# A hybrid mLSTM and gated-delta block on one core: last corrections of a head group behind the next gate's first weight split, later first phases, a sigmoid moved

## The chip, the cores and the metric

The kernel runs on one core of one Trainium2 chip. The metric is the device time of one execution in microseconds (us). The core has a matmul engine (TensorE, PE), a vector engine (VectorE, DVE), an activation engine (ScalarE, ACT), a general engine (GpSimd, POOL) and a sync engine that issues DMAs (SyncE, SP). Each engine works through its own instructions in order.

## The reference

One block of a bidirectional hybrid encoder over 256 tokens of width 2048, in fp32:

```python
mod = c_act @ ada_w + ada_b           # shift, scale, gate of both sub-layers
h = rms_norm(x, norm_mix_w) * (1 + scale_m) + shift_m
proj = h @ w_in                       # a_q a_k a_v a_o a_i a_f | b_qkv b_z b_beta b_a | merge
h_a = bidirectional(mlstm_chunkwise, (q_a, k_a, v_a), ...)          # 4 heads, 512 wide
y_a = (sigmoid(a_o) * rms_norm(h_a)) @ w_branch_a
o_b = bidirectional(gated_delta_chunkwise, (q_b, k_b, v_b), ...)    # 16 heads, 128 wide
y_b = (rms_norm(o_b) * silu(b_z)) @ w_branch_b
x = x + gate_m * ((g_a * y_a + g_b * y_b) @ w_out)
x = x + gate_f * SwiGLU(rms_norm(x) * (1 + scale_f) + shift_f)
```

A final RMSNorm follows. The change touches the gated delta rule of branch B (GDN: 16 heads), its output gate z, and the output gate of branch A, sigmoid(a_o).

## The kernel before, in words

**Every projection** is a product with weights from memory, done in three passes of reduced-precision matmuls. A job loads a weight tile (`raw`, three buffers in all), ACT copies a part of it to `wh`, DVE subtracts to `wl` (three buffers each), and PE adds wh x h-high, wh x h-low and wl x h-high into PSUM. There are two kinds of job. A `tjob` (L195) takes halves of 128x1024: load at L206, wh at L209, wl at L211, twelve 128x512 matmuls at L230 to L232. An `fjob` takes 24 matmuls of 128x256 for a half, with wh at L182 and the matmuls at L187 to L189. A job is a generator that gives one half per step. When a tjob has the argument `early`, its first `early` halves are split at its first step and pinned to the program's order by `order`; other instructions may be moved by the scheduler.

**The GDN** runs over four groups of four heads. For a group, `gdn_invert` inverts 32x32 blocks on DVE: a memset at L687, then steps of a multiplication (L692) and an addition (L698) on the tile uu, which a DMA brings in. Then two pairs of heads run the chain `gdn_phase2`: products p1 to p4 (L743 to L783), then pa, pb and pc (L795, L796, L807), then po (L817 to L822) and a norm. At its last step the chain transposes the result on PE (px, L829), ACT evicts px to obt (L833), and a DMA stores obt to ob_d (L834).

**The order around it.** While a pair's chain runs, `stream` (L875) works off the projections b_job of two heads of the next group, and then `gdn_phase1` of them: vf comes from ACT at L337, PE transposes it to vps at L601, ACT evicts it, and ks follows at L630. The list todo counts down how many pieces later a head's next phase comes. When nothing of the stream is left, `fill(1)` takes the next half from a list of other projections (v, o, q and k of branch A, and the merge gates ma and mb). The tables after, second and last say how many pieces come between two steps of the chain. So these halves are what PE does while a chain waits for DVE or ACT. The gate z of the next group is `z_job`, put at the head of the fills once both pairs are done, with `early` as 0.

**After the last group** the mLSTM of the first two heads runs. For a head, sgo is loaded by POOL (L939), PE sums pden (L950), ACT makes dn from it (L952), PE makes ph (L966), ACT and DVE turn it into hs (L968, L969), ACT squares it (L970) and takes a square root (L972), and DVE scales hs by it and by sgo (L975). Beside it the stored ob_d comes back by POOL's queue (o, L1066, two buffers) and is split by ACT into obh (L1070) and by DVE into obl (L1071); the projection yb consumes these. obh, the mLSTM's dn and the like lie in memory that the GDN's tiles held. The gate a_o is projected by `a_vo` (L375) and evicted by `keep` (L351) with a Sigmoid, stored as o_d, and loaded as sgo. Small PSUM tiles (px, po, pden, ph and so on) take turns in four banks.

Of the kernel before, what the change touches and what calls it, by code (L numbers as in the profile page):

```python
# [9 lines left out]
F32 = mybir.dt.float32  # L10
F32R = mybir.dt.float32r
AF = mybir.ActivationFunctionType
ALU = mybir.AluOpType
# [8 lines left out]
NH_B, DK_B = 16, 128  # L22
# [3 lines left out]
GRP = 4  # L26
# [26 lines left out]
def hybrid_block(ctx: ExitStack, tc: tile.TileContext, xr, nfr, crow, pk_d, cst_d, ada2, ada4, win0, winb, wint, wba, wbb, wo, wgu, wd, out, dbg=None):  # L53
    nc = tc.nc
    V, S, G, PE = nc.vector, nc.scalar, nc.gpsimd, nc.tensor
# [15 lines left out]
    def order(ins, yes=True):  # L71

        return tc.keep_in_program_order(ins) if yes else ins
# [118 lines left out]
                done(o)  # L192
            yield True

    def tjob(name, chunks, xh, xl, done, early=0, by_token=None, steps=1, parts=((0, slice(0, 512)), (1, slice(0, 512)))):  # L195

        raws = {}

        def halves(u, k0):
            if u not in raws:
                raws[u] = raw_tile([P, 4, 512], f"raw_{name}_{u}")
                nc.sync.dma_start(raws[u], chunks[u])  # L206
            wh = st.tile([P, 2, 512], F32R, tag="wh", bufs=3, name=f"wh_{name}_{u}_{k0}")
            wl = st.tile([P, 2, 512], F32R, tag="wl", bufs=3, name=f"wl_{name}_{u}_{k0}")
            order(S.activation(wh, raws[u][:, k0 : k0 + 2], AF.Copy), early)  # L209
            settle()  # L210
            order(V.tensor_tensor(wl, raws[u][:, k0 : k0 + 2], wh.bitcast(F32), ALU.subtract), early)  # L211
            return wh, wl

        todo = [(u, k0) for u in range(len(chunks)) for k0 in (0, 2)]
        made = []
        for i, q in enumerate(todo[:early]):
            made.append(halves(*q))
            if steps > 1 or i == early - 1:
                yield True
        ps = [acc_ps.tile([P, 512], F32, tag="acc", name=f"acc_{name}_{t}") for t in range(2)]  # L220
        last = 4 * len(chunks) - 1
        if by_token:
            todo = todo[:-2]
        for n, (u, k0) in enumerate(todo):
            wh, wl = made.pop(0) if made else halves(u, k0)
            for k in range(2):
                kk = 4 * u + k0 + k
                for t in range(2):
                    c = slice(t * P, (t + 1) * P)
                    order(PE.matmul(ps[t], xh[:, kk, c], wh[:, k], start=kk == 0, stop=False), early and steps > 1)  # L230
                    PE.matmul(ps[t], xl[:, kk, c], wh[:, k], start=False, stop=False)  # L231
                    PE.matmul(ps[t], xh[:, kk, c], wl[:, k], start=False, stop=kk == last)  # L232
            if k0:
                pump()
                if u == len(chunks) - 1:
                    done(ps)
            yield True
            if early and steps > 1:
                if n + early < len(todo):
                    made.append(halves(*todo[n + early]))  # L240
                yield True
        if by_token:
            w = [halves(len(chunks) - 1, k0) for k0 in (0, 2)]
            by_token()
            for i, (t, part) in enumerate(parts):
                if i > 1:
                    ps.append(acc_ps.tile([P, 512], F32, tag="acc", name=f"acc_{name}_{i}"))
                c = slice(t * P, (t + 1) * P)
                o = ps[i][:, : part.stop - part.start]
                for k in range(4):  # L250
                    kk = last - 3 + k
                    wh, wl = (a[:, k % 2, part] for a in w[k // 2])
                    PE.matmul(o, xh[:, kk, c], wh, start=i == 2 and not k, stop=False)
                    PE.matmul(o, xl[:, kk, c], wh, start=False, stop=False)
                    PE.matmul(o, xh[:, kk, c], wl, start=False, stop=kk == last)
                done(t, ps[i], part)
                yield True
# [5 lines left out]
    fills = []  # L263
# [28 lines left out]
    hh = big(bigA, F32R, "hh")  # L292
# [17 lines left out]
    def decay_load(h):  # L310
        al = als[h] = fr.tile([P, 2, T + 8], F32, tag="al", bufs=2, name=f"al{h}")
        order(G.memset(al[:, :, 0:8], 0.0))
        order(G.dma_start(al[:, :, 8:], alpha_d[:, h].partition_broadcast(P)))
# [32 lines left out]
    def keep(dst, fn, name):  # L346

        def done(ps):
            ev = evp.tile([P, 2, 512], F32, tag="ev", bufs=2, name=f"ev_{name}")
            for t in range(2):  # L350
                S.activation(ev[:, t], ps[t], fn)  # L351
            S.dma_start(dst, ev)
        return done
# [5 lines left out]
            S.dma_start(dst, ev)  # L359
        return done  # L360

    def z_job(g, early=0):
        def done(ps):
            szs[g] = evp.tile([P, 2, 512], F32, tag="sz", bufs=1, name=f"sz{g}")
            for t in range(2):
                S.activation(szs[g][:, t], ps[t], AF.Silu)
        return tjob(f"z{g}", [wint[g, u] for u in range(4)], hh, hl, done, early)

    def b_job(h, j):
        return fjob(f"b{h}_{j}", winb[3 * (h - GRP) + j], lambda ps: gdn_conv(h, j, ps))  # L370
# [4 lines left out]
    def a_vo(i, h):  # L375
        return tjob(
            f"{'vo'[i]}{h}", [wint[4 + 4 * i + h, u] for u in range(4)], hh, hl,
            keep((v_d, o_d)[i][h], (AF.Copy, AF.Sigmoid)[i], f"{'vo'[i]}{h}"),
        )

    def m_job(i, g):
# [201 lines left out]
    def gdn_phase1(h):  # L583
# [68 lines left out]
                inst[4 * b : 4 * b + 4].rearrange("x j i -> j x i"), mi[32 * b : 32 * b + 32, :, 32 * b : 32 * b + 32]  # L652
            ), b)

        final = hl_ == GRP - 1
        if h + 2 < NH_B and not final:
            decay_load(h + 2)
        order(G.dma_start(uus[g][16 * hl_ : 16 * hl_ + 16], inst))
        if h + 2 < NH_B and final:
            decay_load(h + 2)  # L660

        cc = ccs[h % NB]

# [211 lines left out]
    def stream(h0):  # L875

        todo = []

        def piece():

            for q in list(todo):
                q[0] -= 1
                if not q[0]:
                    todo.remove(q)
                    next(heads1[q[1]])

        for h in range(h0, min(h0 + 2, NH_B)):
            for j in range(3):
                for _ in b_job(h, j):
                    piece()  # L890
                    yield True
            todo += [[2, h], [4, h]]
        while todo:
            fill(1)
            piece()
            yield True
        while True:
            fill(1)
            yield True
# [3 lines left out]
    def mlstm(h):  # L903
# [56 lines left out]
        for t in range(2):  # L960
            pn = []
            for d in range(2):
                ph = gps(f"ph{h}_{t}_{d}")
                terms = src[d, t]
                for i, (w, s) in enumerate(terms):
                    PE.matmul(ph, w, vt[:, s], start=i == 0, stop=i == len(terms) - 1)  # L966
                pn.append(ph)
            S.activation(hs[:, t], pn[0], AF.Copy, scale=dn[:, t, 0:1])  # L968
            V.scalar_tensor_tensor(hs[:, t], pn[1], dn[:, t, 1:2], hs[:, t], ALU.mult, ALU.add)  # L969
            S.activation(sq, hs[:, t], AF.Square, accum_out=ss[:, t : t + 1])  # L970
            yield
        S.activation(ss, ss, AF.Sqrt, bias=epsc, scale=1.0 / DV_A)  # L972
        V.reciprocal(ss, ss)
        for t in range(2):
# [31 lines left out]
    def invert(g):  # L1006
        gen = gdn_invert(g)
        next(gen)
        fill(4 if g else 6)
        for _ in gen:  # L1010
            fill(1)

    invert(0)
    for g in range(4):
        blocks = gdn_blocks(g)
        next(blocks)
        fill(8)
        next(blocks)
        fill(1)
        pairs = [gdn_phase2(g, p) for p in range(2)]  # L1020
        if g == 3:
            settle()
            sf.close()
            mq["pool"] = pool(sq_, "mq", side="right")
            first2 = [mlstm(h) for h in range(2)]
            for c in first2:
                next(c)
        every[0] = (4, 2, 2, 2)[g]
        for p in range(2):
            pieces = stream(4 * g + 2 * p + 4)  # L1030
            for n in range(1, 10):

                held[0] = n < 4
                if p == 0:
                    next(blocks, None)
                next(pairs[p], None)
                if g == 3 and n == (8, 4)[p]:
                    next(first2[p])
                for _ in range(last[n] if g == 3 else second[n] if p else after[n]):
                    next(pieces)  # L1040
            for _ in pairs[p]:
                pass

            if g < 3:
                while 4 * g + 2 * p + 5 not in heads:
                    next(pieces)
        if g < 3:
            fills.insert(0, z_job(g + 1))
            every[0] = owed[0] = 0
            if asked:  # L1050
                add()
            invert(g + 1)
# [489 lines left out]
```

## Time and profile before

| | |
|---|---|
| time, median of 3 runs | 2056.79 us (2049.5 to 2057.14) |
| the profiled execution | 2056.26 us, span 2054.3 us |
| granted TensorE clock, mean | 0.992 |
| HBM over the span | 467.07 MB read, 236 GB/s |

The span runs from the first to the last instruction that the profiler saw. An engine's busy time is the sum over its instructions; "idle before" is the time in which an engine had nothing running, with the event that ended it. In a line such as "wh_z<-raw_z 128x1024" the tile written stands left of the arrow, the tiles read right of it. Columns of a time line are start in us, duration in us, engine, line, operation, tiles, and in square brackets the idle time before and what released the engine.

### The profile page before, as it was taken

How to read it: one execution, taken by the hardware profiler on the slowest of the kernel's cores; microseconds unless marked ns; L12 is line 12 of the kernel's file. 1: busy time of each engine (PE TensorE's matmuls, PEld its weight loads, DVE VectorE, ACT ScalarE, POOL GpSimd, SP SyncE). 2: the span in 40 equal slices, each digit the busy share in tenths (PEclk: the TensorE clock that was granted, in tenths of full speed). 3: DMA queues.
4: the chain of work that ended last, by engine and by line, in shares of the span. 5: the costliest groups of instructions: out<-in, count | busy, mean ns of one | idle time of the engine just before them, and what ended most of it. 6: DMA issues, size and time to landing. Idle time of an engine off the chain costs nothing.

```text
span 2054.3 us, 27025 instructions
## 1 busy us (share of the span) xinstructions
PE 2017.2 (98%) x10386; PEld 1698.6 (83%) x10386; DVE 1397.7 (68%) x2062; ACT 1027.4 (50%) x1541; POOL 116.6 (6%) x211
## 2 busy tenths in 40 slices
PE   8999999999999999999999999999999999999998
PEld 6878789988997888889787888788888888878886
DVE  5778877877888788866577778756556554555554
ACT  3146647765675667455534444644444444444443
POOL 0001210111011010100100000200000000000000
PEclk9999999999999999999999999999999999999999
DMA  9986666656666666686776877466666665555553
GB/s 400 420 332 209 195 224 227 220 165 212 226 199 221 245 205 226 205 288 260 260 269 254 309 292 289 163 236 237 237 226 234 254 226 187 193 194 196 193 192 136
DMA packets 78962, 485.64 MB, mean 236 GB/s; under 512 B 10585, under 2 KB 15969, under 8 KB 24433
## 3 DMA queue, kind: packets, MB, share of 16 engines
q1 hardware_dynamic: 63216, 450.69, 60.5%
q0 software_dynamic: 8160, 17.88, 3.9%
q10 hardware_dynamic: 7458, 15.36, 2.0%
q8 instruction: 81, 1.33, 0.3%
q14 instruction: 47, 0.39, 0.1%
HBM read 467.07 MB, written 16.82 MB: 236 GB/s over the span
## 4 chain that ended last, share of the span: by engine, by line
PE 86%; DMA 6%; DVE 5%; ACT 1%; issue 1%; POOL 0%; ACTq 0%; SPq 0%; DVEq 0%; POOLq 0%
PE acc_gt L230 4%; PE acc_gt L232 4%; PE acc_gt L231 4%; PE acc_up L232 4%; PE acc_up L231 4%; PE acc_up L230 4%; PE acc_d L230 4%; PE acc_d L232 4%; PE acc_d L231 4%; DMA ra<-ada 3%; PE acc_o L232 3%; PE acc_o L230 3%; PE acc_o L231 3%; PE acc_b L187 2%; PE acc_b L188 2%; PE acc_b L189 2%
## 5 line engine op out<-in xcount | busy, mean ns | idle before, releaser
L211 DVE TENSOR_TENSOR wl_d<-raw_d,wh_d 128x1024 fp32r<-128x1024 f32 x88 | 107.9, 1226 | 119.9 <-ACT wh_d L209 119.9
L211 DVE TENSOR_TENSOR wl_up<-raw_up,wh_up 128x1024 fp32r<-128x1024 f32 x88 | 107.8, 1226 | 111.9 <-ACT wh_up L209 111.9
L211 DVE TENSOR_TENSOR wl_gt<-raw_gt,wh_gt 128x1024 fp32r<-128x1024 f32 x88 | 108.6, 1234 | 89.1 <-ACT wh_gt L209 89.1
L187 PE MATMUL acc_b<-hh,wh_b 128*128 128x256 f32 x576 | 164.7, 286 | 0.0
L209 ACT ACTIVATE wh_d<-raw_d 128x1024 fp32r<-128x1024 f32 x88 | 93.3, 1061 | 139.0 <-PE acc_d L231 134.0
L189 PE MATMUL acc_b<-hh,wl_b 128*128 128x256 f32 x576 | 160.8, 279 | 0.0
L188 PE MATMUL acc_b<-hl,wh_b 128*128 128x256 f32 x576 | 159.6, 277 | 0.0
L209 ACT ACTIVATE wh_gt<-raw_gt 128x1024 fp32r<-128x1024 f32 x88 | 93.3, 1060 | 128.7 <-PE acc_gt L231 77.3
L111 DVE SCALAR_TENSOR_TENSOR ada<-ada,crow 128x2048 f32<-128x2048 f32 x64 | 146.2, 2284 | 10.8 <-DMA ada<-ada 10.8
L209 ACT ACTIVATE wh_up<-raw_up 128x1024 fp32r<-128x1024 f32 x88 | 93.2, 1060 | 118.0 <-PE acc_up L231 84.2
L230 PE MATMUL acc_gt<-wh_gt,hfh 128*128 128x512 f32 x352 | 139.2, 395 | 0.1
L231 PE MATMUL acc_gt<-wh_gt,hfl 128*128 128x512 f32 x352 | 138.3, 393 | 0.0
L232 PE MATMUL acc_gt<-wl_gt,hfh 128*128 128x512 f32 x352 | 137.5, 391 | 0.0
L230 PE MATMUL acc_up<-wh_up,hfh 128*128 128x512 f32 x352 | 136.9, 389 | 0.0
L231 PE MATMUL acc_up<-wh_up,hfl 128*128 128x512 f32 x352 | 136.9, 389 | 0.0
L232 PE MATMUL acc_up<-wl_up,hfh 128*128 128x512 f32 x352 | 136.9, 389 | 0.0
L230 PE MATMUL acc_d<-wh_d,ffh 128*128 128x512 f32 x344 | 134.3, 391 | 0.0
L231 PE MATMUL acc_d<-wh_d,ffl 128*128 128x512 f32 x344 | 134.3, 390 | 0.0
L232 PE MATMUL acc_d<-wl_d,ffh 128*128 128x512 f32 x344 | 133.9, 389 | 0.0
L557 PE MATMUL first<-x,raw 128*128 128x256 f32 x512 | 115.9, 386 | 6.4 <-ACT x L551 6.4
L557 PEld LDWEIGHTS first<-x,raw 128*128 128x128 f32 x512 | 97.3, 192 | 25.1 <-ACT x L551 12.0
L187 PEld LDWEIGHTS acc_b<-hh,wh_b 128*128 128x128 f32 x576 | 108.4, 188 | 1.2 <-issue 0.9
(374 smaller groups left out, 5262.6 us busy)
## 6 DMA issues: line engine op xcount, KB each, us to landing
ada<-ada SPq DMA_DIRECT2D x64, 1024.0 KB, 4.9
raw_gt<-wgu SPq DMA_DIRECT2D x44, 1024.0 KB, 4.9
raw_up<-wgu SPq DMA_DIRECT2D x44, 1024.0 KB, 4.9
raw_d<-wd SPq DMA_DIRECT2D x44, 1024.0 KB, 4.8
raw_b<-winb SPq DMA_DIRECT2D x36, 1024.0 KB, 5.0
ra<-ada SPq DMA_DIRECT2D x32, 1025.0 KB, 15.3
raw<-win SPq DMA_DIRECT2D x16, 1024.0 KB, 14.5
raw_z<-wint SPq DMA_DIRECT2D x16, 1024.0 KB, 5.5
```

The source lines that it names most:

```text
L111: order(V.scalar_tensor_tensor(raw, raw, 1.0, row_c[:, :D], ALU.mult, ALU.mult, accum_out=mod[:, c : c + 1]), room[0][3] > 1)
L187: PE.matmul(o, wh[:, k], hh[:, kk], start=kk == 0, stop=False)
L188: PE.matmul(o, wh[:, k], hl[:, kk], start=False, stop=False)
L189: PE.matmul(o, wl[:, k], hh[:, kk], start=False, stop=kk == KB - 1)
L209: order(S.activation(wh, raws[u][:, k0 : k0 + 2], AF.Copy), early)
L211: order(V.tensor_tensor(wl, raws[u][:, k0 : k0 + 2], wh.bitcast(F32), ALU.subtract), early)
L230: order(PE.matmul(ps[t], xh[:, kk, c], wh[:, k], start=kk == 0, stop=False), early and steps > 1)
L231: PE.matmul(ps[t], xl[:, kk, c], wh[:, k], start=False, stop=False)
L232: PE.matmul(ps[t], xh[:, kk, c], wl[:, k], start=False, stop=kk == last)
L557: PE.matmul(first[o], raw[:, o], x[:, b], start=b == 0 and o % 2 == 0, stop=b == KB - 1 and o % 2 == 1)
```

## The change

Four things are changed.

1. `z_job(g + 1, 1, False)` is started for groups 0 to 2 before the last step of the second pair's chain, so that wh and wl of z's first half are issued ahead of px and obt. The new argument pin leaves these two instructions free to be moved. The chain's next to last step is not advanced in the loop any more for the second pair.
2. The odd heads' first phase comes one piece later: [3, h] and [5, h] for them rather than [2, h] and [4, h].
3. The gate a_o is evicted with Copy rather than Sigmoid; the mLSTM applies the Sigmoid to sgo in place, in front of its square root.
4. decay_load of head 4g + 5, issued at the last head of group g before, is issued in the loop of group g's inversion.

```diff
-    def tjob(name, chunks, xh, xl, done, early=0, by_token=None, steps=1, parts=((0, slice(0, 512)), (1, slice(0, 512)))):
+    def tjob(name, chunks, xh, xl, done, early=0, by_token=None, steps=1, parts=((0, slice(0, 512)), (1, slice(0, 512))), pin=True):
...
-            order(S.activation(wh, raws[u][:, k0 : k0 + 2], AF.Copy), early)
+            order(S.activation(wh, raws[u][:, k0 : k0 + 2], AF.Copy), early and pin)
             settle()
-            order(V.tensor_tensor(wl, raws[u][:, k0 : k0 + 2], wh.bitcast(F32), ALU.subtract), early)
+            order(V.tensor_tensor(wl, raws[u][:, k0 : k0 + 2], wh.bitcast(F32), ALU.subtract), early and pin)
...
-    def z_job(g, early=0):
+    def z_job(g, early=0, pin=True):
...
-        return tjob(f"z{g}", [wint[g, u] for u in range(4)], hh, hl, done, early)
+        return tjob(f"z{g}", [wint[g, u] for u in range(4)], hh, hl, done, early, pin=pin)
...
-            keep((v_d, o_d)[i][h], (AF.Copy, AF.Sigmoid)[i], f"{'vo'[i]}{h}"),
+            keep((v_d, o_d)[i][h], AF.Copy, f"{'vo'[i]}{h}"),
...
-        final = hl_ == GRP - 1
-        if h + 2 < NH_B and not final:
+        if h + 2 < NH_B and hl_ < GRP - 1:
             decay_load(h + 2)
         order(G.dma_start(uus[g][16 * hl_ : 16 * hl_ + 16], inst))
-        if h + 2 < NH_B and final:
-            decay_load(h + 2)
...
-            todo += [[2, h], [4, h]]
+            todo += [[2 + h % 2, h], [4 + h % 2, h]]
...
+        S.activation(so, so, AF.Sigmoid)
         S.activation(ss, ss, AF.Sqrt, bias=epsc, scale=1.0 / DV_A)
...
-        for _ in gen:
+        for i, _ in enumerate(gen):
+            if not i and g < 3:
+                decay_load(4 * g + 5)
             fill(1)
...
-                next(pairs[p], None)
+                if n < 9 or not p or g == 3:
+                    next(pairs[p], None)
...
-            for _ in pairs[p]:
-                pass
             if g < 3:
                 while 4 * g + 2 * p + 5 not in heads:
                     next(pieces)
+                if p:
+                    zj = z_job(g + 1, 1, False)
+                    next(zj)
+            for _ in pairs[p]:
+                pass
         if g < 3:
-            fills.insert(0, z_job(g + 1))
+            fills.insert(0, zj)
```

## The prediction, made before the result

> **What bounds the kernel now.** I read the page's busy line and chain first, then what TensorE (PE) waits for, then the time lines around the places that the change touches.
>
> ```profile
> span 2054.3 us, 27025 instructions
> PE 2017.2 (98%) x10386; PEld 1698.6 (83%) x10386; DVE 1397.7 (68%) x2062; ACT 1027.4 (50%) x1541; POOL 116.6 (6%) x211
> PE 86%; DMA 6%; DVE 5%; ACT 1%; issue 1%; POOL 0%; ACTq 0%; SPq 0%; DVEq 0%; POOLq 0%
> ```
>
> PE works through 98% of the span. The change adds and drops no matmul, so it can gain only where PE stands still, or where PE's clock is cut. The waits of PE, by what released them:
>
> ```profile
> PE vps L601 <- ACT vf L337: 4.0, 5, 2.5
> PE acc_z L232 <- DVE wl_z L211: 3.0, 2, 2.0
> PE acc_z L230 <- ACT wh_z L209: 2.5, 1, 2.5
> PE p L783 <- DVE pt L772: 1.1, 1, 1.1
> PE pa L796 <- DVE UL L732: 0.9, 1, 0.9
> PE pc L795 <- DVE r L808: 0.5, 1, 0.5
> ```
>
> The columns are total us, times, longest. What the edits can reach is the first three rows, under 10 us, or 0.5% of the span. So the idle time to be won is small, and any idle time that the change makes counts as much.
>
> **Part 1, z's first weights ahead of the last corrections.** The longest waits of the first two z rows are these:
>
> ```profile
> 818.64 0.84 ACT L833 ACTIVATE obt<-px,pk 128x256 f32<-128x256 f32 x2 [1.00 <-PE px L829]
> 820.00 1.06 ACT L209 ACTIVATE wh_z<-raw_z 128x1024 fp32r<-128x1024 f32 x1 [0.52 <-ACT obt L833]
> 821.11 0.53 PE L230 MATMUL acc_z<-wh_z,hh 128*128 128x512 f32 x1 [2.51 <-ACT wh_z L209]
> ```
> ```profile
> 642.40 0.19 DVE L692 TENSOR_TENSOR utmp<-uu 64x30 f32<-64x30 f32 x1 [5.48 <-issue]
> 643.25 1.21 DVE L211 TENSOR_TENSOR wl_z<-raw_z,wh_z 128x1024 fp32r<-128x1024 f32 x1
> ```
> ```profile
> 644.51 0.50 PE L232 MATMUL acc_z<-wl_z,hh 128*128 128x512 f32 x1 [1.95 <-DVE wl_z L211]
> ```
>
> Before z3, ACT evicts px to obt and only then splits z's first half: PE idles 2.51. In the changed program's order wh_z stands ahead of obt, so ACT can make it while the pieces before px run, and that wait goes: -2.5. Before z2, DVE's first step of the inversion (L692) waits 5.48 for its input, with wl_z queued behind it: PE idles 1.95. In the changed order the inversion's first instruction stands behind z's first split halves: -2.0. What is late next is the inversion itself, by about two halves of 1.21, with the z matmuls as cover. px's transposes still stand before z on PE; obt comes up to a wh of 1.06 later, and nothing but the later store hangs on it.
>
> A stall here costs more than its length, as the granted clock shows (columns: length, PE busy, clock, DMA share, GB/s):
>
> ```profile
> 555.00:558.60 3.60, 1.15 (x11) 1.00 1.00 385
> 558.60:565.40 6.80, 6.80 (x33) 0.50 0.43 178
> 817.50:821.20 3.70, 1.19 (x7) 1.00 0.32 106
> 821.20:824.90 3.70, 3.70 (x10) 0.54 0.10 18
> ```
>
> Behind z3's wait PE gets 0.54 of its clock for 3.7 us: 3.7 x 0.46 = 1.7 lost. I count that as gone too. Part 1: -2.0 - 2.5 - 1.7 = -6.2. A stretch behind z2 at a cut clock did not occur, so nothing is added there.
>
> The Trainium skill ("TensorE: Matmul & The Clock Gate", part 1, the HAM clock gate) puts the cut after at least one idle window of about 3.4 us. The trace differs on the length: waits of 2.46 and 2.51 were enough here. By the page's length, the 1.7 would not be tied to the wait and part 1 would give -4.5.
>
> **Part 2, odd heads' first phase one piece later (L892).** The one odd head that stalls PE:
>
> ```profile
> 557.11 1.06 ACT L182 ACTIVATE wh_a<-raw_a 128x1024 fp32r<-128x1024 f32 x1 [4.02 <-DMA raw_a<-winb]
> 558.53 0.65 PE L601 MATMUL vps<-cst,vf 128*128 128x128 f32 x2 [2.46 <-ACT vf L337]
> ```
>
> vf stood on ACT behind wh_a, which waited for its weights. With vps a piece later PE comes to the matmuls of that same wh_a, so the wait moves rather than goes. Ends: 0, and -5.9 if it vanishes with its clock cut (2.46 + 6.8 x 0.50). I take 0, by the row at 557.11: the weights land late whoever asks first. What the delay does cost is filler: each of the six streams uses one more half-job, six of 24 matmuls at 0.116 us, some 16.5 us of work that is then missing at the end of group 3 (part 4). Smaller gaps can open beside the chain of each pair where its cover is now thinner; the three short rows of the waits above (1.1, 0.9, 0.5) bound a few such places: 0 to +3, I take +1.5.
>
> **Part 3, decay_load and pin.** POOL's order is the same in both programs: 0. Without the pin the scheduler may place z's splits; the order above is what it made of it.
>
> **Part 4, o's sigmoid moved to the mLSTM (L378, then behind L970).** Evicting o with Copy costs the same pass. Four sigmoids over 128x1024 are new on ACT, 1.06 each by wh_z's row of that size, and ACT is idle half the time; the table loads go from 54 to 53 in the two built programs. What counts is what they wait for, and they meet the thinned end of group 3. The rows there now:
>
> ```profile
> 982.51 0.60 PE L829 MATMUL px<-cst,on 128*128 128x128 f32 x4
> 985.48 0.39 PE L232 MATMUL acc_ma<-wl_ma,hh 128*128 128x512 f32 x1
> 985.71 2.73 PE L950 MATMUL pden<-ones,mdec 128*128 128x1 f32 x24
> 995.49 10.90 PE L966 MATMUL ph<-vt,mdec 128*128 128x512 f32 x24
> ```
> ```profile
> 983.44 0.82 ACT L833 ACTIVATE obt<-px,pk 128x256 f32<-128x256 f32 x2
> 990.25 0.24 ACT L952 ACTIVATE dn<-pden 128x4 f32<-128x4 f32 x2 [3.52 <-DMA ob_d<-obt]
> 998.05 1.06 ACT L1070 ACTIVATE obh<-o 128x1024 fp32r<-128x1024 f32 x1 [4.28 <-DMA o<-ob_d]
> 1011.71 1.28 ACT L351 ACT_TABLE_LOAD   x1
> 1013.00 1.09 ACT L351 ACTIVATE ev_ma<-acc_ma 128x512 f32<-128x512 f32 x2
> ```
> ```profile
> 999.14 1.23 DVE L1071 TENSOR_TENSOR obl<-o,obh 128x1024 fp32r<-128x1024 f32 x1 [4.12 <-ACT obh L1070]
> ```
> ```profile
> 990.80 1.51 POOL L1066 DMA_DIRECT2D o<-ob_d  x2 [63.38 <-ACT dn L952]
> 1000.66 0.76 POOL L1066 DMA_DIRECT2D o<-ob_d  x1 [7.28 <-DVE obl L1071]
> 1014.63 0.53 POOL L939 DMA_DIRECT2D sgo<-o_d  x1 [1.60 <-DVE hs L975]
> ```
>
> Read as a chain: obt, store, dn (6.8 after obt), o loaded (7.8 after dn), obh and obl (10.1 after dn), then the first yb matmul. Before, 60 matmuls of ma (0.23 each by 985.48 to 985.71, 13.7 us) lay on PE between px and yb beside pden and ph. After, none does: px is followed by pden, ph and yb. Call px's start 0. obt now stands behind ma's eviction (1.09) and starts at 1.4, dn at 8.2. PE ends pden at 3.0 (0.36 + 2.60); of twelve ph matmuls at 0.86, three find a free bank (to 5.6), the fourth needs pden's bank and waits for dn: +2.8. The other nine end at 16.2, but obl ends only at 8.2 + 10.1 = 18.3: about +1.9. Together 4.7; if the loads land sooner, 0. I take 4.0.
>
> Then ACT's queue. Times from dn's start: PE starts yb's first half at 10.1, a half is 12 matmuls or 2.75 us, so the fourth half is wanted at 18.4. Its wh stands on ACT behind obh of the fourth o, whose load is issued behind the second obl (11.5) and lands some 6.3 later (17.8): obh 1.05, wh 1.06, first matmul at 19.9, and wl 1.22 for the third at 21.1: +2.3, ends 0.4 and 4. The second sigmoid stands between two table switches (1.28 each) ahead of the sixth half: +0.5, ends 0 and 0.9. A half of the next yb then stands behind the sigmoid of the fourth sgo. Its buffer comes free only behind hs of the second head (before, DVE was waited for there and the load issued at 1014.63, 24.4 after dn); I place it at 25.3. How long such a load takes:
>
> ```profile
> L939 POOL DMA_DIRECT2D sgo<-o_d x4: 528/540/547, 992.3 to 1014.6; - x4
> ...
> DMA to landing us min/median/max: 10.0/13.6/16.9
> ```
>
> At 10.0 it lands at 35.3; sigmoid and wh, 1.06 each, end at 37.4; PE wants it at 10.1 + 8 x 2.75 + 2.8 = 34.9: +2.5, at the maximum +9.4. I take the minimum, since a PE that waits calls up fewer weights beside it. Before, no ACT instruction waited for sgo, only DVE at L975. One more clock cut behind one of these gaps: +1.7, ends 0 and 3.4. Part 4: 4.0 + 2.3 + 0.5 + 2.5 + 1.7 = +11.0, ends about +3 and +22.
>
> The Trainium skill ("ScalarE: Activation LUTs", what ACT_TABLE_LOAD costs) adds a drain of 1.38 us to each switch of the table. The trace does not show it: the load at 1011.71 takes 1.28 and ev_ma starts at 1013.00. By the page the two switches ahead of the sixth half would add some 2.8 more, and the sum would be 2065.
>
> **Sum.** -6.2 + 0 + 1.5 + 11.0 = +6.3. The profiled execution took 2056.26 (span 2054.3 and 2.0 around it), 0.5 under the median of 2056.79, so no correction is made: 2056.3 + 6.3 = 2062.6, said as **2063**. A measurement of this kernel tells about 0.5%, 10.3 us, from no change: 2046.5 to 2067.1.
>
> **Rivals.**
> - *The sgo wait decides (slower).* If the third and fourth sgo land after their 13.6 to 16.9, the last gap is 6 to 9.4 rather than 2.5, with two clock cuts and the first gaps at their upper ends: part 4 is 17 to 22, the time 2069 to 2074. For it: the stretch in which the two loads ran before, whose DMA share is 0.89 (columns: length, busy time and count of PE, PEld, DVE, ACT and POOL, clock, DMA share, GB/s). Against: a PE that waits asks for fewer weights. It decides from a landing of about 13.6 on, where the sum passes +10.
> ```profile
> 1012.00:1040.00 28.00, 28.00 (x133) 23.17 (x132) 19.34 (x23) 16.39 (x22) 1.51 (x3) 1.00 0.89 328
> ```
> - *The end stays covered.* If stores and loads land near their minima, part 4 is about 3, and with -6.2 and part 2 between 0 and -5.9 the time is 2047 to 2055. Against: dn's 3.52 and obh's 4.28 already end on DMAs in the trace, with 13.7 us more on PE.
> - *It doesn't do what it says.* z's early halves need raw and wh buffers that the jobs before still hold; then the waits only move into the pieces before px, part 1 gives 0, and the time is about 2056 with a covered end, 2069 with mine. For it: wh has three buffers only. Against: the three waits of acc_z listed above are those of z0, z2 and z3; z1 has none in the old order, so the supply of weights is not what is short.
> - *Odd heads win.* Part 2 gives -5.9 with the rest as forecast: 2057.
>
> **Chances.** Forecast and its neighbourhood (2055 to 2067, the odd heads' case in it): 0.50. The sgo wait: 0.36. Covered end: 0.10. Nothing of part 1: 0.04, half of it slower. Faster by over 0.5% needs the covered end with the odd heads' gain: 0.05. Slower: 0.37. Same: 0.58. The range is 2050 to 2075: it takes in the slow rival and the upper part of the covered one, and leaves out about 0.15.
>
> **What would show it.** In the profile after: no wait of acc_z on wh_z or wl_z above 0.5 us; no cut clock around 820; pden directly behind px_1, and PE idle before ph and the first yb; ACT waiting for DMA sgo at the new sigmoid, and PE's acc_yb waiting for wh_yb. If PE shows no wait of acc_yb, part 4 is wrong. If vps of head 9 waits no more and no acc_a waits in its place, part 2 is wrong. If the new gaps sum to over 17 us, it was the sgo loads.

## The result, and the profile after

| | before | changed |
|---|---|---|
| median of 18 runs each | 2052.95 us | 2059.79 us |
| lowest to highest | 2049.5 to 2057.73 | 2056.73 to 2063.35 |
| the profiled execution | 2056.26, span 2054.3 | 2059.50, span 2057.6 |

The ratio is 1.0036, with a 95% interval of 1.0028 to 1.0043: slower by 7.4 us (5.7 to 8.8 of 2053). The prediction was +6.3 and 2063; its 2063 stands 3 us above the measured 2059.8 because it was added to a time of before, 2056.3, that is 3.3 above the median found here. The profiled execution of before was that 3.3 us above its own median, so the two traces differ by only 3.2; they are read for places, and the sizes are taken from the timed rounds.

From the changed kernel's page the chain that ended last, and then its waits of PE (total us, times, longest):

```profile
PE 79%; DMA 9%; DVE 8%; ACT 2%; issue 2%; POOL 0%; ACTq 0%; SPq 0%; DVEq 0%; POOLq 0%
```
```profile
PE acc_a L187 <- ACT wh_a L182: 4.1, 1, 4.1
PE p L780 <- DVE pt L769: 3.5, 2, 2.4
...
PE acc_yb L230 <- ACT wh_yb L209: 1.3, 1, 1.3
PE acc_yb L232 <- DVE wl_yb L211: 1.2, 2, 0.7
PE acc_z L232 <- DVE wl_z L211: 1.1, 1, 1.1
...
PE acc_yb L231 <- DVE obl L1077: 0.8, 1, 0.8
PE ph L964 <- ACT dn L950: 0.6, 1, 0.6
...
PE acc_yb L230 <- ACT obh L1076: 0.2, 1, 0.2
```

The long waits of acc_z are gone; the 1.1 left is one wait, z0's, which the change does not touch. In the chain that ended last, PE's share falls from 86% to 79% and DMA's and DVE's rise from 6% and 5% to 9% and 8%. The new waits are acc_a and p in the groups, and acc_yb, ph and obl at the end.

Where the time went can be read from the first z matmul of each group (z1, z2), the last px and the first ya. First the kernel before, then the changed one, on PE's time line:

```profile
441.58 0.48 PE L230 MATMUL acc_z<-wh_z,hh 128*128 128x512 f32 x1
630.51 0.48 PE L230 MATMUL acc_z<-wh_z,hh 128*128 128x512 f32 x1
1121.43 0.39 PE L230 MATMUL acc_ya<-wh_ya,hah 128*128 128x512 f32 x1
```
```profile
452.16 0.48 PE L230 MATMUL acc_z<-wh_z,hh 128*128 128x512 f32 x1
650.10 0.48 PE L230 MATMUL acc_z<-wh_z,hh 128*128 128x512 f32 x1
839.06 0.48 PE L230 MATMUL acc_z<-wh_z,hh 128*128 128x512 f32 x1
995.16 0.60 PE L826 MATMUL px<-cst,on 128*128 128x128 f32 x4
1124.61 0.39 PE L230 MATMUL acc_ya<-wh_ya,hah 128*128 128x512 f32 x1
```

Against 441.58, 630.51, 821.11, 982.51 and 1121.43 the changed kernel is later by 10.6, 19.6, 18.0, 12.7 and 3.2. Part of that is work done earlier: a half of 2.78 more per stream, so 5.6, 11.1 and 16.7 at z1, z2 and z3 (24 and 48 matmuls of 128x512 and 144 of 128x256 more stand ahead of them), and the 60 ma matmuls, 13.7, at px. What is lost is the rest: +5.0 by z1, +8.5 by z2, +1.3 by z3, -1.0 by px, +3.2 by ya. Group 0 and group 1 lose, the stretch from z2 to z3 wins, the end loses 4.2.

### The profile page after: what moved, and what is told of

Read it like the earlier page. It is cut to its first block, busy times and chain, and to the rows that moved or that the text cites. A ratio compares the mean times of both kernels' runs of the same rounds, so it can differ in the third digit from the quotient of the medians.

```text
span 2057.6 us, 27018 instructions
## 1 busy us (share of the span) xinstructions
PE 2016.7 (98%) x10386; PEld 1696.5 (82%) x10386; DVE 1397.7 (68%) x2062; ACT 1029.6 (50%) x1544; POOL 116.7 (6%) x211
## 4 chain that ended last, share of the span: by engine, by line
PE 79%; DMA 9%; DVE 8%; ACT 2%; issue 2%; POOL 0%; ACTq 0%; SPq 0%; DVEq 0%; POOLq 0%
PE acc_gt L230 4%; PE acc_gt L231 4%; PE acc_gt L232 4%; PE acc_up L231 4%; PE acc_up L232 4%; PE acc_up L230 4%; PE acc_d L230 4%; PE acc_d L231 4%; PE acc_d L232 4%; DMA ra<-ada 3%; PE acc_o L232 3%; PE acc_o L231 3%; PE acc_o L230 3%; PE acc_b L187 2%; PE acc_b L189 2%; PE acc_b L188 2%
## 5 line engine op out<-in xcount | busy, mean ns | idle before, releaser
L209 ACT ACTIVATE wh_d<-raw_d 128x1024 fp32r<-128x1024 f32 x88 | 93.3, 1061 | 139.0 <-PE acc_d L231 134.0
L111 DVE SCALAR_TENSOR_TENSOR ada<-ada,crow 128x2048 f32<-128x2048 f32 x64 | 146.1, 2283 | 10.8 <-DMA ada<-ada 10.6
```

The lines of the kernel that those rows point to most:

```text
L111: order(V.scalar_tensor_tensor(raw, raw, 1.0, row_c[:, :D], ALU.mult, ALU.mult, accum_out=mod[:, c : c + 1]), room[0][3] > 1)
```

## The experiments

My theory after the result: z's waits are won, and the end and the odd heads' later phases lose more. The rivals: the sigmoids on sgo alone cost the time, or the early split of z wins nothing since its waits turn up elsewhere. All were timed in five rounds beside the kernel before. "Against before" is the ratio less one, times 2053 us, with its 95% interval.

### Eight kernels: each part with and without the others

The change has three parts that move something: z's early split (z), the later first phases of the odd heads (odd), and the moved sigmoid (sig). Six kernels beside before and the changed one give all eight combinations. decay_load went with whichever file was edited, so kernels made from the changed file carry its move and those made from before (z, odd and sig alone) do not; it was not tried by itself.

**z and odd, no moved sigmoid:**
```diff
-            keep((v_d, o_d)[i][h], AF.Copy, f"{'vo'[i]}{h}"),
+            keep((v_d, o_d)[i][h], (AF.Copy, AF.Sigmoid)[i], f"{'vo'[i]}{h}"),
...
-        S.activation(so, so, AF.Sigmoid)
```


> The changed kernel with o evicted through Sigmoid again and no sigmoid on sgo in the mLSTM. If the sgo sigmoids on ScalarE hold up the weight splits of yb, the waits of acc_yb on wh_yb and wl_yb (3.2 us between 1020 and 1036 in the changed kernel's trace) go, and the time is 2056 to 2058. If only the missing filler between px and yb is at fault, those waits stay and the time is within 1 us of the changed kernel (2059.8).

**z and sig, odd heads at their old places:**
```diff
-            todo += [[2 + h % 2, h], [4 + h % 2, h]]
+            todo += [[2, h], [4, h]]
```


> The changed kernel with the odd heads' first phases at their old places. If the later first phases are what costs (cover gone at the end of group 3, ada rows and weights meeting the chain at worse places), 60 ma matmuls stand between px and yb again, the waits at the end and the new ones of p4 go, and the time is 2049 to 2052. If the later phases cost only the 1.5 us that the prediction gave their groups, and the sgo sigmoids the rest, it is about 2057 to 2058.

**odd and sig, z split late:**
```diff
-                if n < 9 or not p or g == 3:
-                    next(pairs[p], None)
+                next(pairs[p], None)
...
-                if p:
-                    zj = z_job(g + 1, 1, False)
-                    next(zj)
-            for _ in pairs[p]:
-                pass
         if g < 3:
-            fills.insert(0, zj)
+            fills.insert(0, z_job(g + 1))
```
(the rest of the chain is run ahead of the while loop again, as before)

> The changed kernel with z's first half split after the last corrections again, as before. If the early split is worth its two waits and a cut clock, 6 us come on top: 2064 to 2066, with waits of acc_z on wh_z or wl_z of 2 to 3 us. If its gain was lost elsewhere, within 1 us of 2059.8.

**z alone:** the first part of the change's diff (pin, z_job, the loop) put into the kernel before.

> The kernel before with nothing but z's early split. If the early split is worth 4.5 to 6.2 us by itself: 2046 to 2048.5 (before: 2052.95), with no wait of acc_z left at z2 and z3. If the waits only move into other places: 2052 to 2054.

**odd alone:** that one line of the change put into the kernel before.

> The kernel before with nothing but the later first phases of the odd heads. If these alone cost what the runs so far leave to them (new waits of p4 near 400 us, po near 552, weights late near 566, the end of group 3 uncovered), and z's waits of before stay: 2060 to 2066. If they cost only the 1.5 us of the prediction: 2054 to 2056.

**sig alone:** the two lines of the sigmoid put into the kernel before.

> The kernel before with nothing but the sigmoid moved from the eviction of o to sgo. If the moved sigmoid holds up yb's splits as in the changed kernel (3 us), and nothing else happens: 2055.5 to 2057. If it also spares table loads in the groups and the ma cover of before takes up the waits at the end: 2050 to 2053.

| parts in the kernel | median us | ratio and interval | against before, us |
|---|---|---|---|
| z | 2053.54 | 0.9999 (0.9989 to 1.0010) | -0.2 |
| sig | 2053.93 | 1.0005 (0.9996 to 1.0014) | +1.0 |
| odd | 2067.68 | 1.0075 (1.0061 to 1.0089) | +15.4 |
| z, sig | 2059.33 | 1.0024 (1.0014 to 1.0035) | +4.9 |
| z, odd | 2060.17 | 1.0032 (1.0021 to 1.0043) | +6.6 |
| odd, sig | 2070.47 | 1.0078 (1.0065 to 1.0091) | +16.0 |
| all (the changed kernel) | 2059.79 | 1.0036 (1.0028 to 1.0043) | +7.4 |

**The later odd heads are the cost**: +15.4 alone. The waits of PE in that kernel:

```profile
PE acc_a L187 <- ACT wh_a L182: 5.1, 1, 5.1
PE p L783 <- DVE pt L772: 4.4, 2, 2.2
PE acc_z L232 <- DVE wl_z L211: 3.5, 3, 1.5
...
PE ph L966 <- ACT dn L952: 2.2, 1, 2.2
PE acc_mb L232 <- DVE wl_mb L211: 1.9, 2, 1.8
PE p L758 <- DVE pt L750: 1.9, 2, 1.4
PE acc_o L232 <- DVE wl_o L211: 1.8, 1, 1.8
```

Only ph stands at the uncovered end. The other six rows sum to 18.6 us, and all but z0's wait of about 1 us stands in the groups. In the trace of before the same rows, with z3's wait for wh_z, come to 7.9, and vps falls from 4.0 to 1.1; the span is 10.8 us longer.

**z's early split is worth nothing by itself and 9 us beside odd** (15.4 to 6.6, and 16.0 to 7.4). Alone, it does remove z2's and z3's old waits, but its trace shows others:

```profile
PE vps L601 <- ACT vf L337: 6.6, 4, 5.6
PE acc_z L232 <- DVE wl_z L211: 3.0, 3, 1.6
PE acc_ma L232 <- DVE wl_ma L211: 1.8, 1, 1.8
PE ph L966 <- ACT hs L968: 1.7, 1, 1.7
```

The first is head 9's wait for late weights: 2.46 in the trace of before, 5.6 here. The load of these weights was issued at the same time in both (550.99 and 550.93) and took 6.0 us there and 9.2 here; and this profiled execution, 2058.64, is 5.1 above the kernel's median. So the 5.6 is not typical of the kernel. Beside it wl_ma and ph have grown by some 3 us together, and wl_z still makes PE wait, now 1.6 at its longest. Beside odd, the waits that the early split takes away are those of wl_z in z1 and z2 (1.5 and 0.9), of wl_o and of wl_mb (1.8 each), all in the list above for odd alone, 6.0 of the 9 us: the changed kernel's list has wl_z at z0 only, no wl_o, and wl_mb at 0.3. Why it loses with sig (+4.9 against +1.0), which neither of the expected times for z and sig allowed for, the runs don't settle; that kernel's trace has wl_z at 3.2 and wh_yb at 1.6.

**The moved sigmoid costs 1 us or less beside odd**: 0.6 and 0.8, below what the intervals tell; beside z it costs 5.1 (4.9 against -0.2). It is two effects that cancel. Without it, with z and odd, no wait of acc_yb on wh_yb or wl_yb is left (2.5 us in the changed kernel), as expected. But the expected gain does not come: p waits for pt at a second place, and a clock cut of 3.4 us follows that wait. The groups then have more table loads. With the sigmoid at the eviction:

```profile
L611 ACT ACT_TABLE_LOAD x10 | 12.8, 1283 | 0.2
L351 ACT ACT_TABLE_LOAD x7 | 9.0, 1283 | 0.1
```

and in the changed kernel:

```profile
L611 ACT ACT_TABLE_LOAD x9 | 11.5, 1283 | 0.2
L351 ACT ACT_TABLE_LOAD x6 | 7.7, 1283 | 0.1
```

That these loads are what delays the second p was not tried by itself.

The traces of the eight kernels, one each, show where the two effects stand. From px to ya, with 13.7 added where the odd heads are late, PE takes 138.9 us (before), 138.8 (z), 139.0 (odd) and 140.3 (z, odd) without the moved sigmoid, and 143.4 (sig), 144.3 (z, sig), 142.1 (odd, sig) and 143.2 (all) with it. So the loss at the end goes with the sigmoid, 2.9 to 5.5 us in each of the four pairs, and not with the missing cover, whose four pairs give -1.3 to +1.5. Ahead of px the sigmoid's move wins: px comes 2.5 to 5.4 us earlier with it in each of the four pairs.

### The ada rows beside the moved pieces

In the changed kernel's trace, DVE's step of the wait of p4, and ACT's of the wait of acc_a:

```profile
400.36 2.29 DVE L111 SCALAR_TENSOR_TENSOR ada<-ada,crow 128x2048 f32<-128x2048 f32 x1 [3.13 <-DMA ada<-ada]
```
```profile
569.21 2.01 ACT L182 ACTIVATE wh_a<-raw_a 128x1024 fp32r<-128x1024 f32 x2 [4.78 <-DMA raw_a<-winb]
```

The rows of the modulation's second projection (ada) run in the background: a DMA of 1 MB each, then one DVE step of 2.29 us, drawn on every second or fourth piece. Here DVE stands 3.13 us waiting for such a DMA and then works it off, with pt for p4 behind it.

```diff
-        every[0] = (4, 2, 2, 2)[g]
+        every[0] = (0, 0, 2, 2)[g]
```


> The changed kernel with no row of the second projection (ada) drawn in groups 0 and 1; they are done later, so the whole time is not read, only these groups. If the wait of p4 near 401 us is DVE standing behind an ada row that waits for its DMA, and the wait of acc_a near 566 is a weight load that shares the DMA engines with ada rows, both go (6.7 us together with 3 to 5 us of cut clock). If they come from the new order alone, both stay.

Measured: 1.0080 (1.0067 to 1.0093), as the burst at the end makes it. In the groups:

```profile
447.04 0.48 PE L230 MATMUL acc_z<-wh_z,hh 128*128 128x512 f32 x1
635.16 0.48 PE L230 MATMUL acc_z<-wh_z,hh 128*128 128x512 f32 x1
...
1307.48 0.47 PE L1326 MATMUL pxn<-cst,xn 128*128 128x128 f32 x1 [12.92 <-ACT xn L1262]
```

z1 comes 5.1 us and z2 14.9 us earlier than in the changed kernel (452.16, 650.10), for the same matmuls; neither the wait of p4 near 401 nor that of acc_a near 566 is there, and no clock is cut before 988. So what the odd heads' delay ran into in groups 0 and 1 was the ada rows. The 12.92 is where they come back.

### Cover at the end

```diff
+    last2 = (0, 1, 2, 1, 2, 2, 1, 1, 1, 0)
...
-                for _ in range(last[n] if g == 3 else second[n] if p else after[n]):
+                for _ in range((last, last2)[p][n] if g == 3 else second[n] if p else after[n]):
```


> The changed kernel with twelve ma matmuls (2.75 us) held back from ahead of px to behind it, in group 3's second pair. If the missing cover is what makes PE wait for dn and obl at the end, those waits (0.85, 0.75 and 1.03 us) shrink by 1.8 to 2.6 and the time is 2057 to 2058. If the end is set by ScalarE's queue alone, 2059 to 2060; if px's norm is the tighter wait, PE waits ahead of px instead and nothing is won.

Measured: 1.0028 (1.0018 to 1.0037), median 2058.00. That is 1.8 under the changed kernel's median, but the intervals overlap. The waits that it should remove are gone from its list: ph for dn (0.6), yb for obl (0.8) and for obh (0.2). Those of ScalarE's queue stay:

```profile
PE acc_yb L232 <- DVE wl_yb L211: 1.2, 2, 0.7
PE acc_yb L230 <- ACT wh_yb L209: 1.1, 1, 1.1
```

So the missing cover and ScalarE's queue make separate waits, and 2.75 us of cover is enough for the first. From px to ya this trace is no shorter even so: 132.7 us and 10.9 for the 48 ma matmuls done earlier, 143.7 against 143.2 in the changed kernel. Its clock is cut three times there (from 997.3, 1031.5 and 1069.0), against once.

### Moving ada rows for good

```diff
-        every[0] = (4, 2, 2, 2)[g]
+        every[0] = (0, 4, 2, 2)[g]
...
-    every[0] = 2
+    every[0] = 1
     for g in range(4):
         for i, _ in enumerate(y_a(g)):
```

The same edit in three kernels: the changed one, before, and before with z alone.

> The changed kernel with nine of the 48 ada rows moved: none in group 0, fewer in group 1, one for every piece rather than every second in the ya projections. If the waits of p4 near 401, po near 552 and acc_a near 566 with their cut clocks come from ada rows beside them, these go without a burst at the end: 10 to 13 us less than the changed kernel, 2047 to 2050. If the ya stage can't take the rows, waits appear there and it is 2055 or more.

> The kernel before with the same nine ada rows moved. Its one wait beside ada rows is that of head 9's vps (2.5 us and 3.4 of cut clock): 2046 to 2049 if the row's DMA is its cause, 2052 to 2053 if not.

> The kernel before with the early split of z alone and the same nine ada rows moved. Without ada's disturbance the early split shows what it is worth by itself: 4 to 6 us less than the kernel before with the rows moved, if the prediction's first part holds; within 1.5 us of it, if z's waits only move to other places, as they did without the moved rows.

Measured: 1.0030 (1.0020 to 1.0039), 1.0008 (0.9998 to 1.0018) and 1.0005 (0.9995 to 1.0015). None of the gains came. Most of the waits in the groups do go: ya begins at 1109.14, 1108.58 and 1104.95, against 1124.61 and 1121.43. By z2 the changed kernel is then 10.5 us behind the kernel before with the same edit (634.91 against 624.40), which is less than the 11.1 of work done earlier; with the rows in their old places it is 19.6. But ya gives the gain back: it takes 196.3 us from its first matmul to pxn in the changed kernel with the rows moved, against 183.1 in both kernels without that edit. Two rows of its waits of PE, then one of the four waits of pxm on the time line, and last the same transposes in the kernel before:

```profile
PE pxm L1106 <- DVE mg L1096: 4.9, 4, 1.5
...
PE acc_ya L230 <- ACT wh_ya L209: 2.6, 2, 1.3
```
```profile
1183.97 1.37 DVE L1095 TENSOR_TENSOR gta<-gta,acc_ya 128x512 f32<-128x512 f32 x2 [3.15 <-PE acc_ya L232]
1186.09 1.17 PE L1106 MATMUL pxm<-cst,mg 128*128 128x128 f32 x6 [1.47 <-DVE mg L1096]
```
```profile
1155.83 1.03 PE L1100 MATMUL pxm<-cst,mg 128*128 128x128 f32 x8
```

PE waits for mg, but not because DVE is busy with rows: DVE itself stood idle for 3.15 us before, until PE had finished the group of ya that mg needs. In this build the transposes of a group stand directly behind its last matmul (after 96, 192, 288 and 384 matmuls of ya); in the kernel before, 48 matmuls of the next group lie between (144, 240 and 336), and no pxm waits. So the edit changed the order that the scheduler made of ya, in all three kernels. What in the edit does that is not shown. The next run moves fewer rows, and into other places, with z alone:

```diff
-        every[0] = (4, 2, 2, 2)[g]
+        every[0] = (4, 4, 2, 2)[g]
...
-    every[0] = 2
+    every[0] = 1
     drive(steps(mlstm(2), mlstm(3)), 3)
...
     for g in range(4):
+        every[0] = 2 if g else 1
         for i, _ in enumerate(y_a(g)):
```


> The kernel before with the early split of z alone, and only four of the 48 ada rows moved, from group 1 to the yb and the first ya projections, since nine rows moved into all of ya made VectorE late there. If the rows in group 1 are what its lost time (about 9 us between z1 and z2 in the runs with them) is made of, and yb and the first ya have room: 2045 to 2049, below both kernels. If the rows cost as much where they go: 2052 to 2055.

Measured: **0.9977 (0.9968 to 0.9985)**, median 2049.55 against 2054.80 for before on the same chip: 4.7 us faster than before and some 12 faster than the changed kernel, just above the 2045 to 2049 that was expected. Its z2 and ya:

```profile
625.58 0.48 PE L230 MATMUL acc_z<-wh_z,hh 128*128 128x512 f32 x1
...
1107.15 0.39 PE L230 MATMUL acc_ya<-wh_ya,hah 128*128 128x512 f32 x1
```

ya begins 14.3 us earlier than in the trace of before, and pxn 8.7 earlier: in ya PE waits 3.0 us (wh_ya 1.6, pxm 1.4) and its clock is cut once, which the trace of before does not show there. One pxm out of four stands directly behind its group here, and it is the one that waits. By the timed rounds 4.7 is what remains; the trace of before is 3.3 above its median and this one 1.4 under its own. This kernel has both edits; the four rows without the early split weren't tried.

## Why the prediction was right, and where its terms were not

The time lies in the range, the sign and the size of the sum hold (+6.3 against +7.4). But the terms behind it do not. The end was put at +11.0 and shows +4.2 in the traces; the groups were put at -4.7, and if the end is 4.2, some +3 of the timed +7.4 are theirs. Two errors of 7 to 8 us cancelled, so the closeness of the sum is luck.

1. **z's two waits and the cut clock: right as places.** wh_z now runs ahead of obt, and PE goes from px to z without a gap:

```profile
837.07 1.06 ACT L209 ACTIVATE wh_z<-raw_z 128x1024 fp32r<-128x1024 f32 x1 [1.66 <-PE acc_a L188]
...
839.34 0.84 ACT L830 ACTIVATE obt<-px,pk 128x256 f32<-128x256 f32 x2 [0.94 <-PE px L826]
```

The cut clock there is gone too. As a size, -6.2 holds in no combination: -0.2 alone, +3.9 beside sig, -8.8 and -8.6 beside odd. The step assumed that a wait removed is time won whatever else stands in the kernel.

2. **The odd head's wait moves, it does not go: right.** No vps waits over 0.7 any more; acc_a waits 4.1 for that same late weight, and a cut clock follows. The other half of that part, "I take +1.5" for thinner cover in the groups, is **the step that failed**: odd costs +15.4 alone, and the part by z2 alone is +12.3 in its trace (653.88 against 630.51, less 11.1) and +8.5 in that of the changed kernel, where the early split wins some of it back. The bounds were taken from waits already in the profile of before (1.1, 0.9, 0.5), and they don't bound what a piece does that meets an ada row or its DMA at another time. The ada rows were in the profile (64 steps of 2284 ns, 10.8 us of DVE's waiting) and were left out.

3. **The end: the waits where they were said, but too large.** ScalarE waits for sgo as it was said, though for the third load and not the fourth, and POOL's fourth sgo is issued behind a wh_yb of ScalarE:

```profile
1003.12 0.24 ACT L950 ACTIVATE dn<-pden 128x4 f32<-128x4 f32 x2 [4.86 <-DMA ob_d<-obt]
...
1032.51 1.06 ACT L970 ACTIVATE sgo<-sgo 128x1024 f32<-128x1024 f32 x1 [2.15 <-DMA sgo<-o_d]
1033.47 1.04 ACT L209 ACTIVATE wh_yb<-raw_yb 128x1024 fp32r<-128x1024 f32 x1
1034.42 1.04 ACT L970 ACTIVATE sgo<-sgo 128x1024 f32<-128x1024 f32 x1
```
```profile
1029.33 0.53 POOL L937 DMA_DIRECT2D sgo<-o_d  x1 [8.05 <-ACT wh_yb L209]
```

Term by term: ph and the first yb 4.0, measured 1.6 (0.6 + 0.2 + 0.8); the fourth half 2.3 and the sixth 0.5, measured 2.0 (1.3 + 0.7) and 0.5, at these two halves; the fourth sgo 2.5, measured 0. Its load was issued 26.2 after dn (25.3 was said) but landed within 5.1, by the sigmoid's start, rather than in 10. The third was ScalarE's one wait for sgo, 2.15, and PE had halves enough. The added clock cut was not there either: the stretch of 0.50 at this place fell on ph, as one fell on ma there before (columns: length, PE busy, clock, DMA share, GB/s). It stretched the six matmuls of ph from 998.20 to 4.52 us, which is one reason why PE then waited 0.6 for dn and not 2.8; and the second cut of before in this stretch, at 1067, is gone.

```profile
995.40:998.80 3.40, 3.40 (x30) 0.99 0.92 255
998.80:1002.20 3.40, 3.40 (x6) 0.50 0.73 278
```

In all 4.2 of the 11.0. The eight traces put these on the sigmoid; the 4.0 for the missing cover do not show from px to ya when the odd heads alone are late. What the sigmoid's move wins ahead of px, 2.5 to 5.4 us in the traces, is a term that the prediction put at nothing. The rival in which the sgo loads decide did not come about, though its sign did.

4. **The half clock.** Behind the new waits the clock was cut again:

```profile
401.00:404.80 3.80, 1.39 (x12) 1.00 0.27 63
404.80:408.30 3.50, 3.44 (x17) 0.51 1.01 410
```
```profile
568.70:575.50 6.80, 4.72 (x20) 0.50 0.78 287
```

A wait of 2.4 us was enough once more; the second stretch holds the last 1.6 us of the wait for wh_a and goes on for 5.2 us beyond it. The Trainium skill ("TensorE: Matmul & The Clock Gate", part 1, the HAM clock gate) ties the cut to an idle window of about 3.4 us; the waits of 2.4 to 2.5 in this case differ from that. A wait's length alone does not decide here: 1.37 us near 779 in z and odd, and 1.58 near 402 in the run with held cover, were followed by a cut, while the 1.95 before z2 in the trace of before was not. In each of the fourteen traces the cuts begin on a grid of 3.41 us. Between 140 and 1310 us, leaving out stretches of this grid that were cut themselves or hold pden, PE was busy for at most 0.60 of every stretch that a cut followed, and every stretch below 0.46 was followed by one; in between there are both. So what counts is how much of a wait falls into one stretch, and where the grid lies is chance from run to run.

5. **Tables.** ACT's loads at the end take 1.28, and the next instruction starts within 0.02 of their end, so the drain given by the Trainium skill ("ScalarE: Activation LUTs", what ACT_TABLE_LOAD costs), which would have made it 2065, is not seen here.

What stays open: the profiled execution of before is above its median, and the traces can't say where its 3.3 us stand; and why z's early split gains only beside the odd heads' delay is shown by which waits go, not by a run that isolates their cause. Where the sigmoid wins and loses is read from one trace of each kernel, in which a single clock cut more or less is worth up to 1.7 us.

## What to carry to other kernels

When a matmul engine is 98% busy and its remaining waits are short, parts of a reordering do not add up: measure each with and without the others before crediting one. When pieces of work are shifted by one place, look first at what runs in the background by a count of pieces (here 1 MB rows, whose vector step waits in order for its DMA), since the shift moves all of that against the chain. Where a scheduler may move instructions, compare the order of the later stages too: here moving rows out of the groups brought the start of ya forward by 13 to 17 us in the traces, and ya, where transposes had come forward too, lost that again. Four rows moved beside the early split made 4.7 us of a reordering that won nothing alone.

## What the runs showed that was not expected

The same loads of sgo took 10.0 to 16.9 us before and, by the profile of the changed kernel, much less:

```profile
DMA to landing us min/median/max: 4.4/8.1/11.7
```

A landing time taken from one trace was no bound for the next.
